# A streaming encoder step: four stretches rearranged, and layer 0's POOL products given to DVE

## The chip, the cores and the metric

The kernel runs on one core of a Trainium2 chip. The metric is the time of one execution on the device in microseconds (us). Three runs of the kernel before took 2004.25, 2011.17 and 2015.48 us; the median is 2011.17.

Engines by their short names: PE is TensorE (PEld its weight loads), DVE is VectorE, ACT is ScalarE, POOL is GpSimd, SP is SyncE, which here issues nearly all DMAs. Each engine runs its own instructions in the order in which the program gives them, and waits at one whose inputs are not there.

## The reference

Two layers over N = 544 tokens (512 of a new stream, 32 of a running one), 2048 channels. Layer 0 is recurrent, layer 1 is stick-breaking attention with 16 heads.

```python
def rms_norm(x, g):
    x32 = x.astype(jnp.float32)
    y = x32 * lax.rsqrt(jnp.mean(x32 * x32, axis=-1, keepdims=True) + EPS) * g.astype(jnp.float32)
    return y.astype(x.dtype)
...
def rec_layer(x, h0, conv_buf, pool_buf, pos0, g, w_in, conv_w, conv_b, w_r, b_r, w_i, b_i, lam,
              pool_w, pool_scale, w_out):
    h = rms_norm(x, g)
    proj = h @ w_in
    xa, ga, xb, gb = jnp.split(proj, [D_RNN, 2 * D_RNN, 2 * D_RNN + D_POOL], axis=-1)
    xa_c, conv_new = causal_conv(xa, conv_buf, conv_w, conv_b)
    ya, h_new = rg_lru(xa_c, h0, w_r, b_r, w_i, b_i, lam)
    yb, pool_new = pool_mix(xb, pool_buf, pos0, pool_w, pool_scale)
    mixed = jnp.concatenate([ya.astype(x.dtype) * jax.nn.silu(ga),
                             yb.astype(x.dtype) * jax.nn.silu(gb)], axis=-1)
    return x + mixed @ w_out, h_new.astype(x.dtype), conv_new.astype(x.dtype), pool_new.astype(x.dtype)
...
def att_layer_prompt(x, g, w_in, w_out):
    B, T, _ = x.shape
    q, k, v, gt = att_inputs(x, g, w_in)
    ...
    return x + (o.astype(x.dtype) * jax.nn.silu(gt)) @ w_out, k, v
```

`rg_lru` is a gated linear recurrence over time: two gates from small block products, then h = a * h + u. A final `rms_norm` closes both streams. The norm's factor of a token (1/rms) can be applied after a product, since it is one number per token; the kernel does that.

## The kernel before, in words

**Tiles.** Channels lie on the 128 partitions, tokens along the free axis. x is 16 rows (tiles of 128 channels x 544 tokens). A full-precision product is three matmuls of 128x272 (`mm3`, L107 to L110) on operands split into a high and a low half: weights into `wh` (ACT, L203) and `wl` (DVE, L204), data into `xh` (ACT, L230 or L501) and `xl` (DVE, L231 or L502). `raw` (L191 to L196) loads a chunk of six weight rows into a `wraw` buffer through SP.

**Units.** The work goes in units of two output tiles. A `plain_unit` multiplies everything directly: chunks part 0, part 1 and the rest (`XP` rows), each for outputs m = 0 and 1. A `unit` gets the first twelve rows' share with seven products in place of eight, from sums of operands that live in the slots T1 to T4: `make` (L277 to L287) forms T1 to T3 from three loaded quarters (L283 to L285, then L230 and L231), `last` (L294 to L300) forms T4 from a fourth (L299). These sums are made once for each product matrix and then serve all its units.

**Order.** It is written by hand: each unit has numbered stages, and `hooks` hang other work on a stage (0 to 3 are the four chunks, 4 and 5 the rests and outputs of a plain unit; (m, c) lies inside a rest). `store` holds a DMA back for two stages (L318), `run` lets it go. Weight splits and evictions are given high priority, so the scheduler can put them ahead of other operations of an engine. What one engine's order becomes is therefore not that of the text alone.

**Opening** (L471 to L514, L648 to L657). Unit 0 of layer 0's input projection runs while x is loaded. `load_x` loads a row and splits it (L501, L502). The norm needs the sum of squares over all 16 rows: ACT squares a row into an `ev` buffer (L483), and PE sums it over channels with five matmuls of 128x2 a row (`rstd_add`, L137). PE records two for each of them, so a row is ten records. At hook 1 of unit 1 `rstd_sums` (L148 to L158) turns the sums into 1/rms, and at hook 2 `rstd_spread` (L168, L170) spreads it over the partitions for `rbc`.

**Layer 0's recurrence.** For each of 16 tiles `front` and `back` run beside the next unit's matmuls. POOL makes two products of 128x548 and 128x544 there (L607, L620) and copies the last states (L619).

**Output projection** (L772 to L829). Its 24 mixed rows come back from DRAM (`mixd`). Unit 0 is plain; the loads, `makes` and `lastload` for the slots T1 to T3 hang on its stages 4 to (1, 6), and unit 1 is the first with seven products. `x2_out` adds the residual (L805, L806), stores `x2d` and `x2g`, and POOL adds the squares (L123) into `sqacc`.

**Attention, head 0** (L1045 to L1050). The first product unit is plain. On its stages hang the loads and sums of x2g's operands (`one`, `two`, `three`) and the norm: `rstd_sums` at 3, the spread and DVE's copy of it into `rbc` (L1050) at 4.

**End** (L1142 to L1177). The last four rows' products are added to x3, in two token halves; ACT squares (L1164), POOL adds (L1165), and the second half waits for its norm before `finish` scales (L1145) and stores (L1146) 16 tiles.

Of the kernel before, what the change touches and what calls it, by code (L numbers as in the profile page):

```python
# [61 lines left out]
def trunk_step(ctx, tc, xT, w_in_rec, w_out_rec, gates, pool_w, vecs, st_h, st_conv, st_pool,  # L62
# [274 lines left out]
    def rest(src, m, accs, starts, hooks):  # L337
# [3 lines left out]
        for c in range(0, n, step):  # L341
            if c:
                run(hooks, (m, c))
            with tc.high_priority():
                hi, lo = wsplit(raw(src[:, 2 * NS + c:2 * NS + c + step]))
            for j in range(step):
                xh, xl = XP[c + j]
                for acc, hs, st in zip(accs, (H1, H2), starts):
                    mm3(acc, hi[:, j, :], lo[:, j, :], xh[:, hs], xl[:, hs], st and c + j == 0, c + j == n - 1)

    def plain_unit(srcs, out, hooks=None, more=True, early=()):
# [12 lines left out]
        for m in range(2):  # L364
            run(hooks, 4 + m)
            if more:
                rest(srcs[m], m, accs[2 * m:2 * m + 2], (False, False), hooks)
# [88 lines left out]
    with ExitStack() as l0:  # L456
# [15 lines left out]
        for s in (B11, B12, B21, B22):  # L472
            fresh(s)
        xraw = []

        rps = two_banks()
        blocks = token_blocks(0, N)
        sqs = {}
# [10 lines left out]
        def load_x(k):  # L489
            xk = T()  # L490
            nc.sync.dma_start(xk, xT[:, k, :])
            gk = vcol("norm_rec", k)
            if k < 2 * NS:
                j = k % NS
                parts = [(XH[s][:, j, :], XL[s][:, j, :], h)
                         for s, h in zip((B11, B12) if k < NS else (B21, B22), (H1, H2))]
            else:
                hi, lo = fresh_row(k - 2 * NS)
                parts = [(hi, lo, slice(0, N))]
            for hi, lo, h in parts:  # L500
                nc.scalar.activation(hi, xk[:, h], AF.Identity, scale=gk)  # L501
                nc.vector.scalar_tensor_tensor(lo, xk[:, h], gk, f(hi), ALU.mult, ALU.subtract)  # L502
            xraw.append(xk)

        def load_rows(k0, k1):
            for k in range(k0, k1):
                load_x(k)
# [79 lines left out]
        def back(n, c):  # L587
# [19 lines left out]
            nc.gpsimd.tensor_tensor(m_, m_, xc, ALU.mult)  # L607
# [12 lines left out]
            nc.gpsimd.tensor_tensor(hs, hs, g[:, :N], ALU.mult)  # L620
# [17 lines left out]
        def late0():  # L638
# [15 lines left out]
        hk = {0: decay_rates, 1: lambda: box.append(rstd_sums(rps, 0, N, [])),  # L654
# [113 lines left out]
    with ExitStack() as l0b:  # L768
# [25 lines left out]
        def x2_out(u, st):  # L794
# [5 lines left out]
            def out(which, bk, addend):  # L800
# [6 lines left out]
                if which % 2:  # L807
                    store(x2d[:, m, :], x)
                    sq_add(m, x)
# [441 lines left out]
```

## Time and profile before

| | |
|---|---|
| three runs, median | 2011.17 us (2004.25 to 2015.48) |
| the profiled execution: its time | 2008.65 us |
| the profiled execution: its span | 2006.9 us |
| matmul records | 15082 |
| DMA | 257.04 MB, 128 GB/s over the span |
| granted PE clock, mean | 0.98 |

The span runs from the first to the last recorded instruction; 1.75 us of the execution's time lie around it. In the rows that follow a group is `line engine operation out<-in shape xcount | busy us, mean ns | idle time before it and what ended it`. A window row is `from:to length`, then busy time (and instructions) of PE, PEld, DVE, ACT and POOL, the granted PE clock, the DMA share and GB/s. A line of waits is `engine operand line <- what it waited for: us in total, times, longest`. A line of the timeline is `start, length, engine, line, operation`.

### The profile page before, as it was taken

Reading aid. Unit: us, or ns where it says so; the run is one execution under the profiler, and the core shown is the slowest. Engines: PE = TensorE matmul, PEld = TensorE weight load, DVE = VectorE, ACT = ScalarE, POOL = GpSimd, SP = SyncE. Lnnn points to the kernel's source line nnn. Section 1 sums busy time; section 2 is a strip of 40 time slices with the busy share of each in tenths; the row PEclk is TensorE's granted clock in tenths of the full one; section 3 lists DMA queues with packets and bytes.
Section 4 is the critical chain, followed back from the end, with each engine's and each line's share of the span. In section 5 each row is a group of like instructions: output and inputs, shape, how many; then the busy total and the mean of one; then the engine's idle time right before and its main releaser. Section 6 shows DMA issues by size and latency. Waiting matters only on the chain.

```text
span 2006.9 us, 37651 instructions
## 1 busy us (share of the span) xinstructions
PE 1941.0 (97%) x15082; PEld 1919.6 (96%) x15082; DVE 1446.4 (72%) x2318; ACT 919.3 (46%) x1284; POOL 261.6 (13%) x369
## 2 busy tenths in 40 slices
PE   8999999999999889999799999999999999999996
PEld 8999999998999789999799999999999999999996
DVE  4465668669888665556788888888888888874347
ACT  5466666665434443334444453444444444442233
POOL 0021113112010000101111110110111101110013
PEclk8899999999999989999899999999999999999998
DMA  5254434333335654446433343333333333365334
GB/s 181 63 157 144 141 117 137 101 88 103 106 105 179 206 151 141 144 142 212 137 101 102 118 126 103 101 112 116 98 105 107 121 106 101 101 213 183 106 99 148
DMA packets 129951, 257.04 MB, mean 128 GB/s; under 512 B 15920, under 2 KB 40752, under 8 KB 129776
## 3 DMA queue, kind: packets, MB, share of 16 engines
q1 hardware_dynamic: 129696, 254.37, 42.0%
q8 instruction: 118, 1.93, 0.4%
q14 instruction: 57, 0.47, 0.1%
q0 software_dynamic: 80, 0.28, 0.0%
HBM read 217.64 MB, written 36.95 MB: 127 GB/s over the span
## 4 chain that ended last, share of the span: by engine, by line
PE 76%; DVE 12%; issue 5%; DMA 5%; ACT 1%; POOL 0%; SPq 0%; DVEq 0%; ACTq 0%; POOLq 0%
PE pp L108 23%; PE pp L110 23%; PE pp L109 23%; DVE wl L204 3%; DMA wraw<-in_w_in_att 2%; PE pg L137 1%; DMA wraw<-in_w_in_rec 1%; DVE xl L231 1%; DMA T<-x2g 1%; PE pm L109 1%; DVE big L898 1%; PE pm L110 1%; PE pm L108 1%; PE pa L915 1%; DVE e L447 1%
## 5 line engine op out<-in xcount | busy, mean ns | idle before, releaser
L108 PE MATMUL pp<-xh,wh 128*128 128x272 f32 x3180 | 925.4, 292 | 21.0 <-ACT xh L230 10.7
L110 PE MATMUL pp<-xh,wl 128*128 128x272 f32 x3180 | 921.3, 290 | 4.2 <-DVE wl L204 3.9
L109 PE MATMUL pp<-xl,wh 128*128 128x272 f32 x3180 | 921.0, 290 | 1.3 <-DVE xl L231 1.3
L203 ACT ACTIVATE wh<-wraw 128x768 fp32r<-128x768 f32 (+2 forms) x622 | 485.1, 782 | 839.5 <-PE pp L109 603.8
L204 DVE TENSOR_TENSOR wl<-wraw,wh 128x768 fp32r<-128x768 f32 (+2 forms) x622 | 546.2, 881 | 240.1 <-ACT wh L203 237.4
L108 PEld LDWEIGHTS pp<-xh,wh 128*128 128x128 f32 x3180 | 605.2, 191 | 23.7 <-ACT xh L230 11.6
L110 PEld LDWEIGHTS pp<-xh,wl 128*128 128x128 f32 x3180 | 604.2, 190 | 7.0 <-DVE wl L204 6.8
L109 PEld LDWEIGHTS pp<-xl,wh 128*128 128x128 f32 x3180 | 605.0, 190 | 3.2 <-DVE xl L231 2.1
L110 PE MATMUL pp<-xp,wl 128*128 128x272 f32 x1152 | 334.3, 290 | 2.5 <-DVE wl L204 2.2
L108 PE MATMUL pp<-xp,wh 128*128 128x272 f32 x1152 | 332.3, 290 | 3.0 <-ACT xp L230 3.0
L109 PE MATMUL pp<-xp,wh 128*128 128x272 f32 x1152 | 332.1, 289 | 0.0
L108 PEld LDWEIGHTS pp<-xp,wh 128*128 128x128 f32 x1152 | 218.9, 191 | 4.4 <-ACT xp L230 3.3
L110 PEld LDWEIGHTS pp<-xp,wl 128*128 128x128 f32 x1152 | 218.8, 190 | 3.6 <-DVE wl L204 3.6
L109 PEld LDWEIGHTS pp<-xp,wh 128*128 128x128 f32 x1152 | 218.3, 190 | 0.2 <-DVE xp L231 0.2
L447 DVE TENSOR_TENSOR e<-pp,e 128x272 f32<-128x272 f32 x156 | 65.6, 438 | 42.5 <-PE pp L110 37.9
L408 DVE TENSOR_TENSOR e<-pp,e 128x272 f32<-128x272 f32 x184 | 75.4, 430 | 5.6 <-PE pp L110 4.6
L109 PE MATMUL pp<-T,wh 128*128 128x272 f32 x256 | 73.0, 288 | 0.0
L110 PE MATMUL pp<-T,wl 128*128 128x272 f32 x256 | 72.9, 287 | 0.0
L108 PE MATMUL pp<-T,wh 128*128 128x272 f32 x256 | 71.9, 288 | 0.0
L230 ACT ACTIVATE xh<-T 128x544 fp32r<-128x544 f32 x72 | 46.5, 654 | 52.7 <-DVE T L283 18.2
L209 ACT ACTIVATE T<-T 128x544 fp32r<-128x544 f32 (+1 forms) x72 | 45.1, 646 | 44.1 <-DMA T<-in_cv 16.1
L231 DVE TENSOR_TENSOR xl<-T,xh 128x544 fp32r<-128x544 f32 x72 | 51.7, 735 | 12.7 <-ACT xh L230 12.5
(242 smaller groups left out, 2141.3 us busy)
## 6 DMA issues: line engine op xcount, KB each, us to landing
wraw<-in_w_in_att SPq DMA_DIRECT2D x128, 384.0 KB, 3.5
wraw<-in_w_in_rec SPq DMA_DIRECT2D x96, 384.0 KB, 3.4
wraw<-in_w_out_rec SPq DMA_DIRECT2D x64, 384.0 KB, 3.4
wraw<-in_w_in_att SPq DMA_DIRECT2D x64, 256.0 KB, 3.3
wraw<-in_w_in_rec SPq DMA_DIRECT2D x48, 256.0 KB, 3.3
wraw<-in_w_out_att SPq DMA_DIRECT2D x32, 384.0 KB, 4.0
T<-in_xT SPq DMA_DIRECT2D x44, 272.0 KB, 4.6
T<-mixd SPq DMA_DIRECT2D x36, 272.0 KB, 4.5
```

The source lines that it names most:

```text
L108: nc.tensor.matmul(out, wh, xh, start=start, stop=False)
L109: nc.tensor.matmul(out, wh, xl, start=False, stop=False)
L110: nc.tensor.matmul(out, wl, xh, start=False, stop=stop)
L137: nc.tensor.matmul(ps[:, 1, 256 + 2 * c:258 + 2 * c], a[:, st:st + P], ones[:, :2], start=first and c == 0, stop=last and c == n - 1)
L203: nc.scalar.activation(hi, src, AF.Copy)
L204: nc.vector.tensor_tensor(lo, src, f(hi), ALU.subtract)
L209: nc.scalar.activation(a, src, AF.Copy)
L230: nc.scalar.activation(h, src, AF.Copy)
L231: nc.vector.tensor_tensor(l, src, f(h), ALU.subtract)
L408: nc.vector.tensor_tensor(sm[name], acc[p], sm[other], ALU.add)
L447: nc.vector.tensor_tensor(src, bk, addend, ALU.add)
L898: nc.vector.tensor_tensor_scan(inc[:, o:o + w][:, ::-1], s, s, 1.0, ALU.mult, ALU.min)
```

## The change

Five edits, none of which alters what is computed.

1. Opening: rows of x are loaded ahead into the space of slots T1 to T3, which is free until unit 10 (`room`), with the weight chunks between them; `early` also feeds the rest chunks. The splits hang on unit 0's stages. Squares are summed by DVE into `sqacc`, and PE sums over channels once.
2. Output projection: unit 1 is plain as well, and the sums' loads and makes hang on its stages; T4 (`three`) is made at stage 0 of unit 2. The squares are added by DVE.
3. Head 0: `rstd_sums` moves from stage 3 to 1, and the copy into `rbc` goes to ACT, with high priority.
4. End: DVE adds the squares, the last two rows' squares stay apart and are summed by PE, and the 16 last stores are issued by SP and ACT in turn.
5. Layer 0's products m*xc and hs*g go from POOL to DVE.

```diff
-    def rest(src, m, accs, starts, hooks):
+    def rest(src, m, accs, starts, hooks, early=()):
...
-                hi, lo = wsplit(raw(src[:, 2 * NS + c:2 * NS + c + step]))
+                hi, lo = wsplit(early.pop(0) if early else raw(src[:, 2 * NS + c:2 * NS + c + step]))
...
+        room = [xs.tile([P, 3, N], F32, tag=f"{q}{s}", name=nm("xraw")) for s in (T1, T2, T3) for q in ("xh", "xl")]
+
+        def load_rows(k0, k1):
+            for k in range(k0, k1):
+                xraw.append(room[k // 3][:, k % 3, :])
+                nc.sync.dma_start(xraw[k], xT[:, k, :])
+
+        def scale_rows(k0, k1):
...
         def squares(k0, k1):
             for k in range(k0, k1):
-                sqs[k] = ev()
-                nc.scalar.activation(sqs[k][:, :N], xraw[k], AF.Square)
-
-        def add_squares(k0, k1):
-            for k in range(k0, k1):
-                rstd_add(rps, blocks, sqs[k], k == 0, k == KT - 1)
...
-        early = [raw(w_in_rec[0, :, :NS])]
-        load_rows(0, 6)
-        early.append(raw(w_in_rec[1, :, :NS]))
-        squares(0, 5)
-        load_rows(6, 8)
-        early.append(raw(w_in_rec[0, :, NS:2 * NS]))
+                sq_add(k, xraw[k], eng=nc.vector)
+
+        def chunk(m, c):
+            early.append(raw(w_in_rec[m, :, c * NS:min((c + 1) * NS, KT)]))
+
+        early = []
+        load_rows(0, 1)
+        chunk(0, 0)
+        load_rows(1, 6)
+        chunk(1, 0)
+        load_rows(6, 9)
+        chunk(0, 1)
+        load_rows(9, 12)
+        chunk(1, 1)
+        load_rows(12, KT)
+        chunk(0, 2)
+        chunk(1, 2)
+        scale_rows(0, 6)
...
-            nc.gpsimd.tensor_tensor(m_, m_, xc, ALU.mult)
+            nc.vector.tensor_tensor(m_, m_, xc, ALU.mult)
...
-            nc.gpsimd.tensor_tensor(hs, hs, g[:, :N], ALU.mult)
+            nc.vector.tensor_tensor(hs, hs, g[:, :N], ALU.mult)
...
-            1: lambda: (add_squares(0, 5), early.append(raw(w_in_rec[1, :, NS:2 * NS])), load_rows(8, 11), squares(5, 9)),
-            2: lambda: (add_squares(5, 9), load_rows(11, 14), squares(9, 13)),
-            3: lambda: (add_squares(9, 13), load_rows(14, 16), squares(13, 16)),
-            4: lambda: add_squares(13, 16)}, early=early)
+            1: lambda: scale_rows(6, 9), 2: lambda: (scale_rows(9, 12), squares(0, 3)),
+            3: lambda: (scale_rows(12, KT), squares(3, 6)), 4: lambda: squares(6, 9),
+            5: lambda: squares(9, 12)}, early=early)
+        squares(12, KT)
...
-                    sq_add(m, x)
+                    sq_add(m, x, eng=nc.vector)
...
-                    4: lambda: (made_rows(), load(), loads[0]()),
-                    (0, 6): lambda: (makes[0](), loads[1]()),
-                    5: lambda: (makes[1](), loads[2]()),
-                    (1, 6): lambda: (makes[2](), lastload())})
+                    4: lambda: (made_rows(), load())})
+            elif u == 1:
+                plain_unit(srcs, out, {
+                    0: loads[0],
+                    1: lambda: (makes[0](), loads[1]()),
+                    2: lambda: (makes[1](), loads[2]()),
+                    3: lambda: makes[2](),
+                    4: load, 5: lastload})
             else:
                 hk = {2: load}
-                if u == 1:
-                    hk[1] = three
+                if u == 2:
+                    hk[0] = three
...
-                with_hooks(ha, {0: [lambda: pend.append(rows(x2g))], 1: [one, lambda: pend.pop()()], 2: [two],
-                                3: [lambda: box.append(rstd_sums(rps, 0, N)), three],
-                                4: [lambda: nc.vector.tensor_copy(rbc, rstd_spread(rps, box[0]))]})
+
+                def spread_rbc():
+                    with tc.high_priority():
+                        nc.scalar.activation(rbc, rstd_spread(rps, box[0]), AF.Copy)
+                with_hooks(ha, {0: [lambda: pend.append(rows(x2g))],
+                                1: [lambda: box.append(rstd_sums(rps, 0, N)), one, lambda: pend.pop()()],
+                                2: [two], 3: [three],
+                                4: [spread_rbc]})
...
-            nc.sync.dma_start(y[:, m, s], o)
+            queue.dma_start(y[:, m, s], o)
...
-                elif m < KT - 1:
+                elif m < KT - 2:
...
-                    nc.gpsimd.tensor_tensor(sqacc[:, s], sqacc[:, s], sq, ALU.add)
+                    nc.vector.tensor_tensor(sqacc[:, s], sqacc[:, s], sq, ALU.add)
...
-            finish(m, 1, r)
+            finish(m, 1, r, (nc.sync, nc.scalar)[m % 2])
```

PE in the opening, where unit 0's second output begins, before. `ev` holds one row's squares, `pp` are the products, `pg` the norm's sums; x5 is one row of x.

```order
L137 MATMUL pg_117<-ones,ev_158 128x2 x5
L108 MATMUL pp_197<-xh_1_109,wh_292 128x272
L137 MATMUL pg_117<-ones,ev_160 128x2 x5
L109 MATMUL pp_197<-xl_2_110,wh_292 128x272
L110 MATMUL pp_197<-xh_1_109,wl_293 128x272
L108 MATMUL pp_198<-xh_3_111,wh_292 128x272
L109 MATMUL pp_198<-xl_4_112,wh_292 128x272
L137 MATMUL pg_117<-ones,ev_162 128x2 x5
```

PE after the change has one such group, behind unit 1's first 36 products:

```order
L108 MATMUL pp_500<-xh_3_111,wh_542 128x272
L109 MATMUL pp_500<-xl_4_112,wh_542 128x272
L110 MATMUL pp_500<-xh_3_111,wl_543 128x272
L137 MATMUL pg_117<-ones,sqacc 128x2 x5
L108 MATMUL pp_501<-xh_1_109,wh_601 128x272
L109 MATMUL pp_501<-xl_2_110,wh_601 128x272
```

Sixteen groups among unit 0's products became one that reads `sqacc`.

DVE at head 0 before, from the last T1 to T3 sums on. `rs` are the norm's five small numbers per token block, `big` the diagonal tiles that the spread multiplies.

```order
L283 TENSOR_TENSOR T_11024<-T_11024,T_11020 128x544
L151 TENSOR_TENSOR rs_74<-rs_73 128x5
L299 TENSOR_TENSOR T_11117<-T_11117,xh_1575_11086 128x544
L284 TENSOR_TENSOR T_11020<-T_11020,T_11022 128x544
L231 TENSOR_TENSOR xl_1578_11089<-T_11024,xh_1577_11088 128x544
L285 TENSOR_TENSOR T_11022<-T_11024,T_11022 128x544
L231 TENSOR_TENSOR xl_1574_11085<-T_11020,xh_1573_11084 128x544
L152 SCALAR_TENSOR_TENSOR rs_74<-rs_74,rs_71 128x5
L299 TENSOR_TENSOR T_11117<-T_11117,xl_1576_11087 128x544
L231 TENSOR_TENSOR xl_1576_11087<-T_11022,xh_1575_11086 128x544
L153 SCALAR_TENSOR_TENSOR rs_73<-rs_74,rs_73 128x5
```

DVE at head 0 after the change, the same chain and what follows it:

```order
L150 RECIPROCAL rs_73<-rs_72 128x5
L151 TENSOR_TENSOR rs_74<-rs_73 128x5
L152 SCALAR_TENSOR_TENSOR rs_74<-rs_74,rs_71 128x5
L153 SCALAR_TENSOR_TENSOR rs_73<-rs_74,rs_73 128x5
L158 TENSOR_SCALAR big_10932<-ident,rs_73 128x128 x5
L231 TENSOR_TENSOR xp_10957<-T_10871,xp_10956 128x544
L231 TENSOR_TENSOR xp_10961<-T_10873,xp_10960 128x544
L231 TENSOR_TENSOR xp_10965<-T_10875,xp_10964 128x544
L204 TENSOR_TENSOR wl_11160<-wraw_11157,wh_11159 128x512
L231 TENSOR_TENSOR xp_10969<-T_10877,xp_10968 128x544
L283 TENSOR_TENSOR T_10942<-T_10942,T_10938 128x544
```

The norm's chain, spread before among the operand sums, stands in one piece ahead of the first of them (L283).

SP in the output projection before, at the residual's loads from `in_xT` for unit 0. The tiles T from `mixd` of 128x2x272 are the quarters for the operand sums; `x2d` and `x2g` are unit 0's stores.

```order
L798 DMA T_7946<-in_xT 128x544
L798 DMA T_7947<-in_xT 128x544
L237 DMA T_7950<-mixd 128x2x272
L237 DMA T_7952<-mixd 128x2x272
L237 DMA T_7954<-mixd 128x2x272
L326 DMA x2d<-T_7946 128x544
L326 DMA x2d<-T_7947 128x544
L195 DMA wraw_8488<-in_w_out_rec 128x768
L195 DMA wraw_8530<-in_w_out_rec 128x768
L237 DMA T_8013<-mixd 128x2x272
L237 DMA T_8015<-mixd 128x2x272
```

SP at the same place after the change:

```order
L802 DMA T_7875<-in_xT 128x544
L802 DMA T_7876<-in_xT 128x544
L195 DMA wraw_8494<-in_w_out_rec 128x768
L326 DMA x2d<-T_7875 128x544
L326 DMA x2d<-T_7876 128x544
L195 DMA wraw_8496<-in_w_out_rec 128x768
L326 DMA x2g<-T_7966 128x544
L237 DMA T_8065<-mixd 128x2x272
L237 DMA T_8067<-mixd 128x2x272
L237 DMA T_8069<-mixd 128x2x272
L195 DMA wraw_8498<-in_w_out_rec 128x768
```

The quarters' loads moved behind unit 0's stores, with unit 1's weight chunks between them.

More of the change, by code (lines that the diff above doesn't have):

```diff
@@ L366, in plain_unit @@
             if more:
-                rest(srcs[m], m, accs[2 * m:2 * m + 2], (False, False), hooks)
+                rest(srcs[m], m, accs[2 * m:2 * m + 2], (False, False), hooks, early)
             for hf in range(2):
@@ L473, in trunk_step @@
             fresh(s)
+        rps = two_banks()
         xraw = []
-        rps = two_banks()
-        blocks = token_blocks(0, N)
-        sqs = {}
+        room = [xs.tile([P, 3, N], F32, tag=f"{q}{s}", name=nm("xraw")) for s in (T1, T2, T3) for q in ("xh", "xl")]
[4 more added lines that the diff above has]
+        def scale_rows(k0, k1):
+            for k in range(k0, k1):
+                xk, gk = xraw[k], vcol("norm_rec", k)
+                if k < 2 * NS:
+                    j = k % NS
+                    parts = [(XH[s][:, j, :], XL[s][:, j, :], h)
+                             for s, h in zip((B11, B12) if k < NS else (B21, B22), (H1, H2))]
+                else:
+                    hi, lo = fresh_row(k - 2 * NS)
+                    parts = [(hi, lo, slice(0, N))]
+                for hi, lo, h in parts:
+                    nc.scalar.activation(hi, xk[:, h], AF.Identity, scale=gk)
+                    nc.vector.scalar_tensor_tensor(lo, xk[:, h], gk, f(hi), ALU.mult, ALU.subtract)
@@ L1140, in trunk_step, with finish @@
         pend.pop()()
-        def finish(m, hf, r):
+        def finish(m, hf, r, queue=nc.sync):
             s = (H1, H2)[hf]
@@ L1145, in finish @@
             nc.vector.scalar_tensor_tensor(o, o, vcol("norm_final", m), r, ALU.mult, ALU.mult)
-            nc.sync.dma_start(y[:, m, s], o)
+            queue.dma_start(y[:, m, s], o)
         for hf, s in enumerate((H1, H2)):
+            accs = [sqacc]
             for m in range(KT):
@@ L1161, in trunk_step @@
                     nc.scalar.activation(sqacc[:, s], x3[m][:, s], AF.Square)
-                elif m < KT - 1:
+                elif m < KT - 2:
                     sq = e()
                     nc.scalar.activation(sq, x3[m][:, s], AF.Square)
-                    nc.gpsimd.tensor_tensor(sqacc[:, s], sqacc[:, s], sq, ALU.add)
+                    nc.vector.tensor_tensor(sqacc[:, s], sqacc[:, s], sq, ALU.add)
                 else:
-                    last = T()
-                    nc.scalar.activation(last[:, s], x3[m][:, s], AF.Square)
-                    accs = [sqacc, last]
+                    accs.append(T())
+                    nc.scalar.activation(accs[-1][:, s], x3[m][:, s], AF.Square)
                 if hf == 1 and m >= 8:
```

23 lines of the change are left out of this document (3 added, 20 removed).

## The prediction

> **What bounds the kernel now.** I read the page first, for the busy shares and the chain that ended last.
>
> ```profile
> span 2006.9 us, 37651 instructions
> PE 1941.0 (97%) x15082; PEld 1919.6 (96%) x15082; DVE 1446.4 (72%) x2318; ACT 919.3 (46%) x1284; POOL 261.6 (13%) x369
> ```
>
> TensorE (PE) is busy 97% of the span, so little seems left. But busy is not fast. The windows of 25 us tell more, by the number of matmuls in each and by the granted clock (the last figures of a row are clock, DMA share and GB/s).
>
> ```profile
> 25.00:50.00 25.00, 25.00 (x166) 25.00 (x167) 8.73 (x20) 12.13 (x23) 0.19 (x1) 0.77 0.35 116
> 50.00:75.00 25.00, 25.00 (x157) 25.00 (x156) 5.26 (x14) 6.69 (x12) 0.00 (x0) 0.73 0.17 52
> 700.00:725.00 25.00, 17.89 (x93) 16.50 (x93) 16.97 (x28) 9.47 (x14) 0.00 (x0) 0.75 0.58 171
> 725.00:750.00 25.00, 25.00 (x202) 25.00 (x201) 15.87 (x23) 10.30 (x15) 2.90 (x2) 1.00 0.44 133
> 975.00:1000.00 25.00, 13.85 (x85) 13.64 (x86) 22.21 (x42) 9.92 (x15) 2.10 (x3) 0.66 0.18 56
> 100.00:300.00 200.00, 200.00 (x1599) 200.00 (x1598) 123.49 (x192) 131.67 (x172) 39.18 (x49) 1.00 0.48 139
> ```
>
> A good stretch does 202 matmuls in 25 us, 0.1238 us each; that is my unit of account. Three places fall short: the opening (clock 0.77 and 0.73 though PE is busy all the time), the start of the output projection about 700 us, and head 0 of the attention about 975 us. The end is the fourth place. Elsewhere PE runs at its rate, and only PE time removed shortens the span.
>
> **The opening.** These are two PE groups between 7 and 76 us, one burst of L137, the end of the spread that closes the stretch, two windows of 2 us in it, and a single burst of ten L137 records at head 0 with the window behind it.
>
> ```profile
> L108 PE MATMUL pp<-xh,wh 128*128 128x272 f32 x72 | 24.4, 351 | 7.3 <-ACT xh L501 7.3
> L137 PE MATMUL pg<-ones,ev 128*128 128x2 f32 x160 | 23.2, 270 | 0.0
> 19.01 1.73 PE L137 MATMUL pg<-ones,ev 128*128 128x2 f32 x10
> 75.88 0.31 PE L170 MATMUL pg<-big,ones 128*128 128x32 f32 x2
> 8.00:10.00 2.00, 2.00 (x9) 1.80 (x9) 2.00 (x6) 2.00 (x6) 0.00 (x0) 1.00 1.03 403
> 24.00:26.00 2.00, 2.00 (x10) 2.00 (x10) 0.00 (x0) 0.00 (x0) 0.00 (x0) 0.50 0.00 0
> 960.55 1.17 PE L137 MATMUL pa<-ones,sqacc 128*128 128x2 f32 x10
> 962.00:972.00 10.00, 10.00 (x82) 10.00 (x81) 6.89 (x13) 5.84 (x9) 0.00 (x0) 1.00 0.96 301
> ```
>
> PE works from 7.25 to 76.19 us, 68.9 us, on 264 products (192 of unit 0: 16 rows, two outputs, two halves, three products; and unit 1's first 72), 160 L137 records and the spread. The products alone are 264 x 0.1238 = 32.7. L137 at full clock is 160 x 0.117 = 18.7 (ten in 1.17). The spread, ten records as well, is about 1.2, and the slow first matmuls (9 in 2 us at the start) cost about 2.3 more. Together 54.9; the missing 14.0 is half clock without an idle gap, as in the window 24 to 26, behind groups like that at 19.01. One burst of ten at 960.55 is followed by ten microseconds at 1.00, so ten alone don't lower the clock. After the change there is one burst of ten. PE's work is then 32.7 + 1.2 + 1.2 + 2.3 = 37.4; begun at 7.25 as before it ends at 44.6, a gain of 31.5 if nothing waits.
>
> What could wait is the burst on sqacc, since DVE now adds the squares. These rows price DVE's work ahead of it:
>
> ```profile
> L502 DVE SCALAR_TENSOR_TENSOR xl<-T,vec,xh 128x272 fp32r<-128x272 f32 x24 | 10.3, 495 | 4.8 <-ACT xh L501 4.8
> L204 DVE TENSOR_TENSOR wl<-wraw,wh 128x768 fp32r<-128x768 f32 x4 | 3.8, 954 | 2.4 <-ACT wh L203 2.4
> L204 DVE TENSOR_TENSOR wl<-wraw,wh 128x512 fp32r<-128x512 f32 x2 | 1.4, 692 | 13.2 <-ACT wh L203 13.2
> L502 DVE SCALAR_TENSOR_TENSOR xp<-T,vec,xp 128x544 fp32r<-128x544 f32 x2 | 1.5, 780 | 0.1
> L283 DVE TENSOR_TENSOR T<-T,T 128x544 f32<-128x544 f32 x3 | 2.2, 724 | 7.5 <-DMA T<-mixd 7.5
> ```
>
> DVE has 10.3 for xl, 3.0 for four xp rows, about 5.2 for unit 0's weights and 1.9 for unit 1's first two, and 15 adds of 0.64 to 0.72 (L283 has their shape), 10 to 11: 30 to 31 from about 7, so 37 to 38.4 without a pause. PE reaches the burst at 7.25 + 2.3 + 228 x 0.1238 = 37.8. I take 1.5 us of waits, there and at the borders between weight chunks, where a schedule by hand from these prices leaves DVE 1 to 2 us: **30** gained. Bounds: 32, and 22 if each of the five borders costs 2 us, which is what DVE would need for two or three operations out of turn.
>
> [...]
>
> **The output projection.** PE's waits between 690 and 724, DVE's longest, and the stretch from the first to the last of these gaps:
>
> ```profile
> PE pp L108 <- ACT xh L230: 10.4, 3, 4.6
> PE pp L108 <- DVE T L806: 1.0, 1, 1.0
> PE pp L110 <- DVE wl L204: 0.8, 1, 0.8
> DVE T L283 <- DMA T<-mixd: 7.5, 2, 4.1
> 690.60:722.40 31.80, 19.04 (x95) 17.38 (x94) 22.32 (x37) 14.11 (x21) 1.87 (x1) 0.79 0.57 168
> ```
>
> Unit 1's operand sums (L283 to L285, L230, L231) wait for loads from mixd. In 31.8 us PE does 95 matmuls, worth 11.8: 20.0 lost, 12.8 in gaps and the rest at half clock. After the change unit 1 is a plain unit on rows that exist, and loads and sums go to its hooks, one unit earlier than their use. It needs 288 matmuls for 270: -2.2. At unit 2 the sums of T4 wait for the last load behind x2d's stores on SP; my trace by hand gives about 2. So 20.0 - 2.2 - 2 = **16**. Upper bound 18; lower 6, if waits like the 7.5 and some 4 us of slow matmuls behind them come back at unit 2. The square adds go to DVE at 0.7 each in the stretch behind, where DVE is at 15.9 of 25: nothing.
>
> **The norm copy at head 0.**
>
> ```profile
> PE pa L168 <- issue: 11.8, 1, 11.8
> PE pp L108 <- DVE T L449: 2.0, 1, 2.0
> 978.44 0.16 DVE L151 TENSOR_TENSOR rs<-rs 128x5 f32<-128x5 f32 x1
> 983.75 1.06 DVE L158 TENSOR_SCALAR big<-ident,rs 128x128 f32<-128x128 f32 x5
> 972.30:997.20 24.90, 11.07 (x66) 10.95 (x66) 22.35 (x42) 9.90 (x15) 2.10 (x3) 0.66 0.17 54
> ```
>
> The 11.8 put down to issue is PE holding the spread until L158, whose small ancestors stand between L283, L299 and L231 on DVE (order rows above). The 24.9 us hold 54 products (6.7) and the spread (1.1): 17.1 lost. After the change L137 comes after 36 matmuls, the chain L150 to L158 stands in one piece, and ACT copies rbc. The operand work of 0.7 each does not shrink: DVE is at 22.4 of 24.9 here, and the T2 operands, behind the x2g loads, are ready about 980.5 by hand, when PE could want them at 977 to 979. I subtract 4: **13**. Upper 16; lower 6, if that DVE queue still ends last.
>
> **The end.**
>
> ```profile
> PE pa L137 <- POOL sqacc L1165: 2.5, 1, 2.5
> L1145 DVE SCALAR_TENSOR_TENSOR big<-big,vec,rbc 128x272 f32<-128x272 f32 x6 | 3.9, 684 | 0.0
> 1988.28 0.42 DVE L1159 TENSOR_TENSOR big<-big,pp 128x272 f32<-128x272 f32 x1
> 1988.63 1.97 DVE L1145 SCALAR_TENSOR_TENSOR big<-big,vec,rbc 128x272 f32<-128x272 f32 x3
> 1999.50 2.54 DVE L1145 SCALAR_TENSOR_TENSOR big<-big,vec,pa 128x272 f32<-128x272 f32 x6
> 1995.93 4.75 SPq L1146 DMA_DIRECT2D out_y<-T  x10
> 2000.78 3.12 SPq L1146 DMA_DIRECT2D out_y<-big  x6
> ```
>
> The 2.5 is not POOL's alone: DVE's last additions stand behind L1145s of 0.66 each (three in 1.97), against 0.42 where POOL is idle (six in 2.54). In the last half 13 adds, at 0.42 as L1159 has it, come to DVE (+5.5), and 16 L1145 get up to 0.24 cheaper (-3.8): 1.7 lost, or less where other DVE work is eased too. Sixteen stores take 7.9 us to issue, 0.49 each, against DVE's 16 x 0.42 = 6.8; two queues leave 1.1. The sum over POOL's last add, 2.5, goes in part. **1**, between -3 (no relief from POOL, the 2.5 stays) and +4 (the 2.5 and the 1.1 whole).
>
> [...]
>
> **POOL's products in layer 0.**
>
> ```profile
> L608 DVE SCALAR_TENSOR_TENSOR ev<-big,ev 128x548 f32<-128x548 f32 x8 | 5.8, 730 | 27.2 <-ACT ev L606 27.2
> L619 POOL COPY ho<-T x16: 187/188/1003, 102.1 to 486.0; 128x2 f32<-128x2 f32 x16
> ```
>
> From 100 to 300 us, eight units, DVE is idle 76.5, 9.6 a unit. m*xc (0.72) falls in the 3.4 that DVE waits before L608; hs*g (0.72) stands behind POOL's copy of ho (0.19 to 1.0), with L449 and the next wl behind it. At most 2.5 of 9.6: **0**, from -2 to +3 for the few full stretches.
>
> **Sum.** 30 + 16 + 13 + 1 + 0 = 60 off the profiled execution's 2008.65: 1948.7. That execution lies 2.5 below the median of the runs, 2011.17, so by the median 1951. I say 1949, nearer to the sum's own basis. The terms' bounds add to 22 + 6 + 6 - 3 - 2 = 29 and 32 + 18 + 16 + 4 + 3 = 73.
>
> **The rivals.** First: the half clock has another cause than the L137 groups. [...] Then the opening's 14.0 stay, the gain is 46, the time 1963. For it: no run here separates them; against it: the window 24 to 26 comes behind L137 groups, and the 200 us from 100 on, without them, are at 1.00. Second: new waits take the old ones' place where the rearranged loads stand, at unit 2 and at head 0, since SP and DVE work in order and DVE is nearly full there: 6 + 6 for 16 + 13, 1966. For it: 22.4 of 24.9 on DVE; against: the chain of five small operations no longer waits between them. Third, slower: DVE's wait for POOL at hs*g holds the next wl. It decides once a unit's waits pass the 9.6 us of DVE idle less 1.4 of new work, 8.2; to turn the sum past +10 us it must cost PE 70 / 16 = 4.4 a unit, a wait of 12.6 where the longest copy shows 1.0; at 4.6 a unit the time is 2011 - 60 + 74 = 2025. Fourth: the gains are hidden by something that the profile does not show (about 2009); against it, all four are gaps or slow matmuls of the engine that sets the span.
>
> **How the numbers follow.** Forecast 0.74 (1937 to 1960), the first rival 0.09, the second 0.11, the third 0.02, the fourth 0.04. A measurement of this kernel can tell about 0.5%, 10 us, from no change. Faster 0.93, same 0.04, slower 0.03. The range from 1936 to 1972 leaves out the last two and the tails.
>
> **What would show it.** Right: the window 25 to 50 with over 195 matmuls at clock 1.00 and L168 of the first spread ending about 45; no wait over 2 us at units 1 and 2 of the output projection, now 31 us earlier, about 660 to 695; the spread at head 0 with no wait over 2 us; and out_y issues on two queues. Wrong: clock under 0.9 after 15 us, PE waiting for sqacc by over 3 us, waits <-ACT xh L230 at unit 2, or PE waits <-DVE wl in layer 0 that recur in each unit.

## The result, and the profile after

The changed kernel takes 1948.85 us (median of 4 runs, 1947.40 to 1951.53), the kernel before 2009.39 (4 runs, 2004.25 to 2015.48). The ratio is 0.970, with a 95% interval from 0.967 to 0.973. Forecast were 1949 us and a range from 1936 to 1972. The sum came out; its terms less so. (One later execution of the changed kernel took 3107.76 us at a mean granted clock of 0.56, a slow state of the core, and is left out everywhere below.)

To see where the time came from I set the two timelines side by side by products, not by time. PE does 13764 products into `pp` before and 13782 after (18 more in the output projection's unit 1). The n-th product of one kernel is the n-th of the other up to there, and behind it, counted from the end. The difference of their start times is what has been gained so far:

| place | start before, us | gained up to it | gained in the stretch ahead | forecast |
|---|---|---|---|---|
| behind the opening (product 500) | 108.7 | 31.0 | 31.0 | 30 |
| the output projection's unit 1 (product 4750) | 690.2 | 35.9 | 4.9 | 0 |
| behind the output projection | 899.8 | 49.8 | 13.9 | 16 |
| behind head 0 | 1051.2 | 56.7 | 7.0 | 13 |
| the last products' start | 1921.7 | 56.1 | -0.6 | 0 |
| the span's end | 2006.9 | 57.2 | 1.1 | 1 |

The stretch called layer 0 below runs from product 500 to 4750; its last 288 products are the output projection's unit 0.

(The profiled execution of the changed kernel is the slowest of its four runs, 1951.53, span 1949.7; hence 57.2 here and 60.5 between the medians.)

The page's first lines:

```profile
span 1949.7 us, 37295 instructions
PE 1908.4 (98%) x14962; PEld 1886.8 (97%) x14962; DVE 1469.1 (75%) x2390; ACT 915.6 (47%) x1281; POOL 176.6 (9%) x294
```

The windows of 25 us that answer to those of before:

```profile
25.00:50.00 25.00, 25.00 (x203) 24.82 (x202) 21.63 (x56) 15.44 (x27) 1.05 (x3) 1.00 0.34 95
50.00:75.00 25.00, 25.00 (x202) 25.00 (x201) 19.34 (x31) 19.11 (x26) 2.00 (x5) 1.00 0.36 103
650.00:675.00 25.00, 23.34 (x185) 23.00 (x184) 14.06 (x21) 9.29 (x14) 0.00 (x0) 1.00 0.69 222
925.00:950.00 25.00, 21.95 (x151) 21.76 (x152) 24.20 (x39) 11.94 (x18) 3.47 (x2) 0.86 0.38 118
```

The opening now runs at its rate: 203 matmuls where 166 stood, clock 1.00. The output projection has no half clock any more. Head 0 (925 to 950) still has some, 0.86. PE's waits over the whole span, the larger ones:

```profile
PE pp L108 <- ACT wh L203: 7.4, 2, 7.1
PE pp L110 <- DVE wl L204: 4.8, 7, 1.1
PE pp L108 <- DVE T L449: 3.1, 1, 3.1
PE pg L108 <- ACT T L209: 2.2, 3, 1.2
PE pa L137 <- DVE sqacc L1179: 2.2, 1, 2.2
PE pp L108 <- ACT xp L230: 2.0, 1, 2.0
PE pp L108 <- DVE T L810: 1.7, 1, 1.7
```

The 11.8 put down to issue is gone, as are the 10.4 <-ACT xh L230. The 3.1 <-DVE T L449 stands at head 0. The opening's burst and the spread behind it:

```profile
38.28 1.28 PE L137 MATMUL pg<-ones,sqacc 128*128 128x2 f32 x10
44.00 1.05 PE L168 MATMUL pg<-big,ones 128*128 128x128 f32 x8
44.89 0.31 PE L170 MATMUL pg<-big,ones 128*128 128x32 f32 x2
```

The spread ends at 45.20, against 76.19 before and the forecast's "about 45"; PE reached the burst at 38.3 and did not wait for `sqacc`.

### The profile page after: what moved, and what is told of

Read it like the earlier page. It is cut to its first block, busy times and chain, and to the rows that moved or that the text cites. A ratio compares the mean times of both kernels' runs of the same rounds, so it can differ in the third digit from the quotient of the medians.

```text
span 1949.7 us, 37295 instructions
## 1 busy us (share of the span) xinstructions
PE 1908.4 (98%) x14962; PEld 1886.8 (97%) x14962; DVE 1469.1 (75%) x2390; ACT 915.6 (47%) x1281; POOL 176.6 (9%) x294
## 4 chain that ended last, share of the span: by engine, by line
PE 76%; DVE 12%; DMA 6%; issue 4%; ACT 2%; POOL 0%; SPq 0%; DVEq 0%; POOLq 0%; ACTq 0%
PE pp L108 23%; PE pp L110 23%; PE pp L109 23%; DVE wl L204 4%; DMA wraw<-in_w_in_att 2%; DVE big L906 1%; DMA T<-mixd 1%; DMA T<-x2g 1%; DVE xl L231 1%; PE pm L109 1%; PE pm L110 1%; PE pm L108 1%; ACT wh L203 1%; PE pa L923 1%; DVE e L447 1%
## 5 line engine op out<-in xcount | busy, mean ns | idle before, releaser
L204 DVE TENSOR_TENSOR wl<-wraw,wh 128x768 fp32r<-128x768 f32 (+2 forms) x619 | 541.4, 878 | 187.3 <-ACT wh L203 180.5
L230 ACT ACTIVATE xh<-T 128x544 fp32r<-128x544 f32 x72 | 46.6, 655 | 53.0 <-DVE T L283 15.8
L231 DVE TENSOR_TENSOR xl<-T,xh 128x544 fp32r<-128x544 f32 x72 | 50.5, 721 | 12.4 <-ACT xh L230 12.3
```

The costliest lines, as they stand in the source:

```text
L204: nc.vector.tensor_tensor(lo, src, f(hi), ALU.subtract)
L230: nc.scalar.activation(h, src, AF.Copy)
L231: nc.vector.tensor_tensor(l, src, f(h), ALU.subtract)
```

## The experiments

Each stretch's gain is read by products, as in the table above, against the kernel before. Most are single executions. The kernel before took 2010.54 us beside `open_alone`, `wide`, `out_alone` and `norm_alone`, 2013.87 beside `pool_alone`, `no_pool`, `end_alone` and `norm_early`, 2014.03 (median of 7) beside `pool_dummy` and `norm_mix`, 2010.58 (median of 11) beside the last two; single executions of it lie between 2004.25 and 2020.36, so the readings by products carry the argument, not the times.

**open_alone**: the opening's lines of the diff, nothing else.

> The kernel before with the opening's edit alone. Theory: the opening gains 31 us by itself (PE's 264th product ends at about 45 us instead of 76) and nothing later moves, so the span is 2006.9 - 31 = 1976. Rival: part of what the whole change gained in the opening hangs on another edit, or the earlier start runs into other waits in layer 0, so the span is above 1980.

Measured: 1985.87 us, span 1984.2. The opening itself gained 30.8, so the term stands by itself. But 8 of it were given back behind: 3.7 in layer 0, 0.3 in the output projection, 0.5 at head 0 and 3.7 in the attention behind it, where the clock stays at 1.00 and PE is idle for 7.8 us instead of 4.6. What happens in layer 0 is to be seen in two windows around the same wait of 1.7 us <-DVE big (L584, L588 in the changed text), the kernel before first, then open_alone.

```profile
330.00:340.00 10.00, 8.34 (x67) 8.12 (x66) 7.63 (x12) 6.83 (x10) 2.79 (x2) 1.00 0.50 141
```

```profile
300.00:310.00 10.00, 8.31 (x52) 7.94 (x51) 7.08 (x11) 6.52 (x9) 1.90 (x2) 0.83 0.53 133
```

The idle time is the same, 1.7 us. In one kernel the clock stays at 1.00, in the other it falls, and 15 matmuls (1.9 us) are lost on top. So the rival was right as to the span: an earlier start meets the same waits at another moment, and the price of a wait is not fixed. The last section shows on what it depends.

**wide**: the L137 matmuls of the opening with 48 moving columns, not 2.

```diff
-            nc.tensor.matmul(ps[:, 1, 256 + 2 * c:258 + 2 * c], a[:, st:st + P], ones[:, :2],
+            nc.tensor.matmul(ps[:, 1, 256 + wd * c:256 + wd * (c + 1)], a[:, st:st + P], ones[:, :wd],
...
-                rstd_add(rps, blocks, sqs[k], k == 0, k == KT - 1)
+                rstd_add(rps, blocks, sqs[k], k == 0, k == KT - 1, 48)
```

> The kernel before with one number changed in the opening: the norm's L137 matmuls have 48 moving columns, not 2 (48 equal sums for one). Theory: the half clock comes from matmuls that hardly occupy the array; with 48 columns the clock stays near 1.00 from 15 to 76 us, the records take the same 0.117 us each, and the spread ends 14 us earlier, at about 62; span 1993. Rival: the half clock has another cause (the weight loads of L137, or the traffic of the opening): the windows stay at 0.73 to 0.77, the spread ends at 76 or later, span 2007 or more.

Measured: 1998.13 us, span 1996.4; the opening gained 11.9. Its windows:

```profile
14.00:30.00 16.00, 16.00 (x113) 16.00 (x112) 8.31 (x30) 8.76 (x18) 0.00 (x0) 0.79 0.50 165
25.00:50.00 25.00, 25.00 (x214) 25.00 (x213) 9.18 (x18) 13.95 (x25) 0.19 (x1) 1.00 0.35 108
50.00:75.00 25.00, 25.00 (x203) 25.00 (x202) 12.00 (x24) 9.48 (x16) 1.40 (x3) 1.00 0.23 64
```

From 25 us on the clock is 1.00 where it was 0.77 and 0.73, with the same 160 records. They do not stand in the same places: with this edit the scheduler put the first 40 behind product 36 in one piece, where the kernel before has groups of ten behind products 36, 37, 41 and 45. So the run by itself does not part the columns from the order. Two stretches of 3.41 us with nearly equal work do, before first, then `wide`, each with the stretch that follows it (why 3.41, the last section says):

```profile
29.68:33.09 3.41, 3.41 (x31) 3.41 (x31) 1.28 (x6) 1.06 (x2) 0.00 (x0) 1.00 0.37 68
33.09:36.51 3.42, 3.42 (x18) 3.42 (x17) 0.92 (x2) 1.68 (x4) 0.00 (x0) 0.50 0.96 359
```

```profile
28.01:31.42 3.41, 3.41 (x31) 3.41 (x31) 2.06 (x5) 2.34 (x6) 0.00 (x0) 1.00 0.47 94
31.42:34.83 3.41, 3.41 (x30) 3.41 (x30) 1.03 (x3) 1.59 (x4) 0.00 (x0) 1.00 1.01 375
```

In both first stretches 10 products start; beside them 20 records of two columns in the one, 19 of 48 columns in the other. Half clock follows the first and not the second, so the two moving columns lowered the clock. Between 14 and 30 us `wide` is still at 0.79: there stands the piece of 40, and in 3.41 us without any product 48 columns do not hold the clock either.

```profile
14.15 3.94 PE L137 MATMUL pg<-ones,ev 128*128 128x48 f32 x33
```

**out_alone**: the output projection's lines and the squares on DVE.

> The kernel before with the output projection's edit alone (unit 1 plain, sums on its stages, squares on DVE). Theory: its gain is its own: 13 to 14 us at equal products, as in the whole change, span 1993. Rival: the forecast's 16 holds for the edit alone and the other edits took 2 of it, span 1991; or the gain needs the others, span above 1998.

Measured: 1994.20 us, span 1992.5; 13.9 gained in the stretch by equal products. The first theory holds. The waits that remain, in this kernel from product 4750 (690.3 us) on:

```profile
PE pp L108 <- DVE T L806: 1.6, 1, 1.6
PE pp L110 <- DVE wl L204: 1.6, 2, 1.2
```

**norm_alone**: head 0's lines.

> The kernel before with head 0's edit alone. The whole change gained 7 us there where I forecast 13. Theory: the missing 6 are the edit's own (T loads land late, DVE then is full, the first unit's evictions L449 stand behind the sums): 7 us here too, with a wait <-DVE T L449 of about 3 us, span 2000. Rival: another edit takes them (squares on DVE ahead of the chain, or the earlier arrival): 11 to 13 us here, span 1995.

Measured: 2005.64 us, span 2003.9. Head 0 gained about 9, from 4.2 behind to 4.5 ahead. That lies between the two expectations, and the waits there are others than in the whole change:

```profile
PE pa L137 <- POOL sqacc L123: 1.7, 1, 1.7
PE pp L108 <- ACT xh L230: 1.4, 1, 1.4
PE pp L108 <- ACT wh L203: 0.4, 1, 0.4
```

No wait for L449, and half clock for one stretch of 3.4 us alone, behind the 1.7 (959.15 to 962.57, clock 0.50). So the 3.1 us of the whole change do not belong to the edit as such. This kernel was also 2.1 us later than the kernel before already at product 250, where the two programs are the same; see the last section.

**pool_alone**: L607 and L620 on DVE.

> The kernel before with the two products of layer 0's recurrence on DVE and nothing else. The whole change gained 4.9 us between the opening and the output projection, where I forecast 0. [...] Rival: the gain comes from the other arrival times after the opening's edit; then 0 to 1 here, span 2006, or a loss.

Measured: 2005.47 us, span 2003.8; I had expected 2002, and 4 to 6 us as this edit's own gain. Layer 0 gained 5.6 up to product 4500, in three steps: 2 us about 330 us, 2 about 460 and 1.4 about 495, where PE's waits <-DVE big L584 and <-DVE wl L204 had been. 2.0 were given back in the output projection, 1.6 of them ahead of product 4750. So the gain is this edit's own, and the rival falls. How POOL costs DVE time is in these rows, POOL's product and the DVE operation beside it in the kernel before, then the same DVE stretch in this one:

```profile
310.24 1.59 POOL L607 TENSOR_TENSOR big<-big,ev 128x548 f32<-128x548 f32 x1 [2.46 <-ACT big L597]
...
310.52 1.89 DVE L231 TENSOR_TENSOR xl<-T,xh 128x544 fp32r<-128x544 f32 x1
```

```profile
310.61 0.72 DVE L607 TENSOR_TENSOR big<-big,ev 128x548 f32<-128x548 f32 x1
311.25 0.72 DVE L231 TENSOR_TENSOR xl<-T,xh 128x544 fp32r<-128x544 f32 x1
```

DVE's own operation took 1.89 us beside POOL's product, and 0.72 without; it ended 0.58 us behind POOL's, as if it had stood still for the rest. Doing the product itself costs DVE 0.64 here, running beside POOL's cost it 1.17. That is not so beside every product: from 80 to 640 us POOL made 32 in the kernel before, ten DVE operations were slowed beside them, by 9 us in all, and L449, which reads PSUM, took its 0.43 beside them too. In `pool_alone` and in the changed kernel no DVE operation is slowed there.

**pool_dummy**: the changed kernel with two products more on POOL in each of layer 0's tiles, into a scratch tile that nobody reads; they are extra work.

```diff
+            nc.gpsimd.tensor_tensor(scr, xc[:, :N], rbc, ALU.mult)
             nc.vector.tensor_tensor(m_, m_, xc, ALU.mult)
...
+            nc.gpsimd.tensor_tensor(scr, g[:, :N], rbc, ALU.mult)
             nc.vector.tensor_tensor(hs, hs, g[:, :N], ALU.mult)
```

> The changed kernel with two products of 128x544 more on POOL in each of layer 0's sixteen tiles, into a scratch tile that nobody reads. Theory: POOL's products slow DVE while they run (a DVE operation beside one took 1.89 us in the kernel before, 0.72 without), so layer 0 loses the 5 to 9 us again that the edit gained there: span 1955 to 1959, waits <-DVE wl and <-DVE big back. Rival: the gain came from the products' results being there earlier on DVE; products that nobody waits for cost nothing: span 1949 to 1951.

Measured: 1953.52 us, span 1951.7. From product 500 to 4000 it lost 0.3 where the changed kernel gained 5.6, and 1.7 already before product 500. PE's waits <-DVE big and <-DVE wl are back, smaller (1.7 and 0.8 between 80 and 600 us; the changed kernel has none there). The theory holds for the place: products that nobody reads cost 6 us there, so it was not the results' earlier arrival. The span, 1951.7, lies under the 1955 expected: it is 2.0 above the first profile of the changed kernel and 7.3 above its second (below). The difference is head 0, which gained 10.2 here and 7.0 and 9.8 in those; the output projection gained 13.6.

**no_pool**: the whole change without those two products.

> The whole change without the two products of layer 0 on DVE (they stay on POOL). The opening's edit alone gave back 3 us of its 31 in layer 0. Theory: without POOL's products on DVE this comes back: the span is 1949.7 + 5 to 8 = 1955 to 1958, with waits of PE <-DVE wl and <-DVE big in layer 0. Rival: the products' place is indifferent (my forecast's 0): 1949 to 1951.

Measured: 1953.53 us, span 1951.8. Layer 0 lost 2.0 in place of gaining 4.9, and the waits <-DVE big and <-DVE wl are back (2.9 and 2.8 between 80 and 600 us), so the theory holds there, at 7 us. The span, 1951.8, misses the 1955 to 1958 expected: 2.1 of the 7 are left against the first profile of the changed kernel and 7.4 against its second (below).

**end_alone**: the end's lines.

> The kernel before with the end's edit alone. Forecast 1 us, the whole change showed 1 there. Theory: about 1 here, span 2005.9, DVE without a gap up to the last addition as before. Rival: with POOL gone DVE's scalings take 0.42 and not 0.66, and the end gains up to 4, span 2003.

Measured: 2004.35 us, span 2002.6, of which 2.7 were gained in the opening, whose program is that of before; 1.6 are left for the end and the scatter of the attention. The first theory holds, within a scatter of half a microsecond: in five runs of the kernel before with other edits the same stretch moved by -0.5 to +0.2. In the changed kernel the last scalings beside no POOL work take the shorter time, and DVE has no gap up to the last sum all the same:

```profile
1933.34 0.92 DVE L1158 SCALAR_TENSOR_TENSOR big<-big,vec,rbc 128x272 f32<-128x272 f32 x2
1934.16 0.44 DVE L1173 TENSOR_TENSOR big<-big,pp 128x272 f32<-128x272 f32 x1
1934.51 0.92 DVE L1158 SCALAR_TENSOR_TENSOR big<-big,vec,rbc 128x272 f32<-128x272 f32 x2
1936.70 0.16 DVE L148 TENSOR_SCALAR rs<-pa 128x3 f32<-128x3 f32 x1 [1.28 <-PE pa L137]
```

Two in 0.92, or 0.46, where three took 1.97. From the last products to L148, behind the last sum, the changed kernel takes 0.5 us longer all the same, the additions on DVE included; from L148 to the end it takes 13.0 in place of 14.6, since the last stores now go out on two queues.

**norm_early**: the changed kernel with head 0's nine loads for the sums ahead of the four rows.

```diff
-                with_hooks(ha, {0: [lambda: pend.append(rows(x2g))],
-                                1: [lambda: box.append(rstd_sums(rps, 0, N)), one, lambda: pend.pop()()],
+                with_hooks(ha, {0: [one, lambda: pend.append(rows(x2g))],
+                                1: [lambda: box.append(rstd_sums(rps, 0, N)), lambda: pend.pop()()],
```

> The changed kernel, with the nine loads for head 0's operand sums issued ahead of the four last rows' loads and one stage earlier. Theory: the 6 us that head 0 gained less than forecast come from late loads: DVE stands idle for them and is then full when the first unit's evictions (L449) are due, PE waits 3.1 us and runs 5 us at half clock. With earlier loads the wait falls under 1 us and the gain there goes from 7 to 10 or 12; span 1945. Rival: DVE's sums are the bound whatever the loads do, or the rows that the running unit needs now land late: no change or slower, 1949 to 1955.

Measured: 1946.66 us, span 1944.8. Head 0 gained 10.1, the wait for L449 and the half clock are gone, and a wait of 2.7 <-ACT xp L230 is new: the rows land late. Both expectations are right in part.

**norm_mix**: two groups of the sums' loads first, then the rows, then the third group.

```diff
-                with_hooks(ha, {0: [lambda: pend.append(rows(x2g))],
-                                1: [lambda: box.append(rstd_sums(rps, 0, N)), one, lambda: pend.pop()()],
-                                2: [two], 3: [three],
+                with_hooks(ha, {0: [loads[0], loads[1], lambda: pend.append(rows(x2g))],
+                                1: [lambda: box.append(rstd_sums(rps, 0, N)), loads[2], lambda: pend.pop()()],
+                                2: [*makes, lastload], 3: [three],
```

> The changed kernel with head 0's loads in a third order: two of the three groups for the operand sums ahead of the four last rows, the third behind. Theory: both waits at head 0 (3.1 us <-DVE T L449 with the rows first, 2.7 <-ACT xp L230 with all sums first) are late loads on SP's one queue; between the two orders both shrink, head 0 gains 12 of the forecast's 13 or more, span 1942 to 1944. Rival: SP's queue is full there, one of the two waits always stays at 2 to 3 us: span 1944.8 to 1950.

Measured: 1945.33 us (4 runs, 1943.65 to 1946.26), ratio to the kernel before 0.965, interval 0.963 to 0.967; span 1943.1. The waits at head 0 shrank to three of 0.6 or less:

```profile
PE pp L108 <- ACT xp L230: 0.6, 1, 0.6
PE pp L109 <- DVE xp L231: 0.6, 2, 0.4
PE pp L109 <- DVE xl L231: 0.6, 1, 0.6
```

Head 0 gained 10.3, less than the 12 expected: over the whole stretch PE is still idle for 2.8 us, and one stretch of 3.4 us at half clock behind the first of these waits (920.01 to 923.42, clock 0.50) cost 1.7 more.

**best**: norm_mix, and unit 0's two residual rows in the output projection loaded at stage 2 instead of 4.

> The changed kernel with head 0's loads in the mixed order and, in the output projection, unit 0's two residual rows loaded two stages earlier. Theory: PE's wait of 1.7 us for a PSUM bank (<-DVE T L810) stands behind these late loads; it goes, so the time is 1 to 2 us under the mixed order's 1945.3: 1943 to 1944.5, ratio to the kernel before about 0.965. Rival: the earlier loads push back the mixed rows on SP's queue, a wait <-ACT T L230 takes the place: 1945 to 1947.

Measured: 1946.51 us (4 runs), ratio 0.967, interval 0.966 to 0.969; span 1943.7. The wait <-DVE T L810 is gone, and 0.6 each <-ACT T L230 and <-DVE T L231 came in its place: the rival. The output projection gained 16.0, but the stretch ahead, where the loads now stand, 4.8 in place of norm_mix's 6.4. It is not shown to be faster than norm_mix.

**after_again**: the changed kernel once more, on the same chip.

> The changed kernel itself, once more beside the one above on the same chip: 1947 to 1952, ratio to the kernel before 0.967 to 0.973. A second profile of it shows how much of the ledger by products differs from run to run: within 1 us in the opening if the clock stays at 1.00 there, where the kernel before moved by up to 3.

Measured: 1946.29 us (median of five runs, 1945.59 to 1947.49), ratio 0.967, interval 0.966 to 0.969; span 1944.4. So neither `best` nor `norm_mix` is shown to beat the changed kernel: their intervals overlap with this one. In this profile head 0 gained 9.8, not 7.0. PE's waits there in the first profile, and windows of 4 us behind the first of them:

```profile
PE pp L108 <- DVE T L449: 3.1, 1, 3.1
PE pp L108 <- ACT wh L203: 0.4, 1, 0.4
```

```profile
924.00:928.00 4.00, 0.85 (x6) 0.66 (x5) 4.00 (x8) 1.66 (x4) 0.00 (x0) 0.87 0.66 231
928.00:932.00 4.00, 4.00 (x19) 4.00 (x19) 4.00 (x7) 2.05 (x4) 2.53 (x2) 0.50 0.19 70
932.00:936.00 4.00, 4.00 (x27) 4.00 (x27) 4.00 (x7) 2.33 (x4) 0.94 (x1) 0.78 0.57 165
```

The same in this profile, waits and then windows of 6 us:

```profile
PE pp L108 <- DVE T L449: 2.0, 1, 2.0
PE pp L108 <- ACT xh L230: 1.4, 1, 1.4
PE pp L108 <- ACT wh L203: 0.4, 1, 0.4
```

```profile
924.00:930.00 6.00, 5.26 (x42) 5.29 (x43) 6.00 (x12) 3.48 (x6) 3.48 (x2) 1.00 0.17 61
930.00:936.00 6.00, 4.58 (x36) 4.36 (x36) 6.00 (x10) 2.42 (x4) 4.90 (x1) 1.00 0.39 122
```

Together PE waits about as long, 3.5 and 3.8 us. In one piece of 3.1 us it is followed by half clock: 46 matmuls from 928 to 936, worth 5.7 us, in 8. In two pieces of 2.0 and 1.4 it is not. `norm_early` has a single wait of 2.7 us and no half clock behind it, so the number of pieces does not decide it (last section).

## Why the prediction was right, step by step

**The opening** (30, measured 31.0 in the whole change and 30.8 alone) was right in mechanism and size. The rival that the half clock has another cause fell with `wide`: the same records with 48 columns gave back 12 of the 14 us that I had put down to it, and at equal work per stretch half clock follows the narrow records alone. PE shows as 100% busy in the rows all the while: 25.00 of 25.00 us in the kernel before's windows at 0.77 and 0.73.

**The output projection** (16, measured 13.9 in the whole change and 13.9 alone) had its mechanism right: no half clock is left in the stretch, and PE's idle time there fell from 12.8 to 3.1. I had subtracted 2 for new waits; 1.7 <-DVE T L810 and 1.4 <-DVE wl L204 came. The first is not new in kind (1.0 <-DVE T L806 stood there before), nor is the second (0.8): I had counted both old ones as gone. That is 1 of the missing 2; the other stays open.

**Head 0** (13, measured 7.0 and 9.8 in two profiles) is the mis-sized term. The chain of the norm no longer waits, as forecast: the burst comes after 36 products and the spread 26 later without a gap. I subtracted 4 for the operand sums. Of the 17.1 us lost before, 10 are still lost in the one profile and 7 in the other. Of these PE's idle time makes 5.1 and 5.0, half clock 3.0 and nothing; 2 us in each are not accounted for. The largest wait comes since DVE stands idle for the sums' loads (2.5 us up to 917.6, and several shorter waits ahead) and then is full when the first unit's evictions are due, 924 to 927. My step "T2 operands ready about 980.5" looked at the sums alone, and left out that L449 stands in the same queue and that a wait of 3 us can bring half clock behind it (here 3.1, and clock 0.50 from 928 to 932). `norm_early` and `norm_mix` show that the order of the loads decides which of the waits comes; even with all of them at 0.6 or less 10.3 were gained, so 13 was too much for this edit in any order that was run.

**The end** (1, measured 1.1 and about 1.6 alone): right in size, and nearly in its parts. The two queues gave 1.6 where I had 1.1; the work up to the last sum cost 0.5, where I had 1.7 lost on DVE and part of the 2.5 of waiting won back. That wait is still there, as 2.2 <-DVE sqacc L1179.

**POOL's products** (0 with a range from -2 to +3, measured in layer 0 as 4.9 and 5.9 in two profiles of the whole change and 4.0 alone): the step that failed is "at most 2.5 of 9.6: 0". I added DVE's new work and did not subtract what DVE had lost beside POOL, though the same effect carried my end term (0.66 against 0.42 for a scaling). In a stretch with idle time that does not show; in the full stretches at 330, 460 and 495 us it was 1.4 to 2 us each. What DVE loses is in the row of 1.89 us against 0.72; by what mechanism, no run shows. That the gain is DVE's time and not the results' arrival is shown by `pool_dummy`. How much of it stays in the span is not settled: 3.1 in `pool_alone`, 2.1 or 7.4 by `no_pool`, 2.0 or 7.3 by `pool_dummy`. That something stays is likely: `no_pool` and `pool_dummy` took 1953.5 in their one execution each, and the nine executions of the changed kernel that are compared here took 1945.59 to 1951.53.

So the total was near by luck in part: 4.9 too little for POOL's products met 6 too much for head 0 and 2 too much for the output projection.

## What to carry to other kernels

A PE that is 100% busy can still run at half clock (3.42 of 3.42 us busy at 0.50, with 18 matmuls where the stretch ahead had 31): count matmuls per window and read the granted clock, and keep tiny matmuls in one burst (of ten records in the changed opening, whose windows stand at 1.00). POOL work beside a DVE that is full is not free: the DVE operation shown lost 1.17 us beside a product of 1.59. Where a stretch is full, give DVE the product (5.6 us in layer 0 in `pool_alone`). When parts of a change are added up, compare timelines by product number: it shows each part's gain in that execution to a tenth of a microsecond, and what the next stretch gives back. One execution is not enough for it: head 0's gain differed by 2.8 us between two profiles of the same kernel.

## What the runs showed of the hardware that I had not expected

The price of a PE wait depends on when it falls. A wait of 1.7 us cost 1.7 in the kernel before and about 3.5 in `open_alone`. The traces show why. In each of the fourteen every change of the granted clock, between 1.00 and 0.50, lies on one grid of 3.41 us (in the kernel before those at 19.44, 29.68, 33.09, 39.92 and 50.16 us are 3, 1, 2 and 3 times 3.41 apart), and this grid lies elsewhere against the program's start in each execution (29.68 us is on it before, 28.01 in `wide`). Two stretches of the grid around that wait, before first, then `open_alone`:

```profile
330.05:333.46 3.41, 1.97 (x16) 1.74 (x14) 3.41 (x6) 1.51 (x2) 0.55 (x1) 1.00 0.53 163
333.46:336.88 3.42, 3.21 (x25) 3.21 (x26) 3.42 (x6) 2.25 (x4) 0.25 (x1) 1.00 0.42 120
```

```profile
299.98:303.40 3.42, 1.73 (x12) 1.36 (x12) 3.42 (x6) 1.51 (x2) 0.55 (x1) 1.00 0.43 129
303.40:306.81 3.41, 3.41 (x17) 3.41 (x17) 3.41 (x6) 1.88 (x3) 0.00 (x0) 0.50 0.44 115
```

In the kernel before the wait falls into two stretches of the grid, 14 matmuls start in the first, and nothing follows. In `open_alone` it falls into one, 10 start, and the next stretch runs at half clock, which costs half of 3.41, 1.7 us. Over all fourteen traces, in the 5924 stretches in which nothing but products of 128x272 and L137 records of two columns starts (a full stretch holds 28 products): fewer than 10 products, and half clock always followed; 13 or more, and full clock always followed; from 10 to 12 both occur. So in these traces it is the products started in a stretch that count, and a wait, or groups of tiny matmuls, cost more when they take enough of one stretch. At head 0 2.4 of the 3.1 us fell into one stretch with 6 products; 2.0 and 1.4 fell into two with 13 and 14; `norm_early`'s 2.7 was cut by the grid into 1.9 and 0.8.

The kernel before is unsteady for the same reason. Four kernels here have its opening unchanged, with PE's operations in the same order, and their product 250 stands at -0.1, -2.1, 0.0 and +2.7 us against the first profile (`out_alone`, `norm_alone`, `pool_alone`, `end_alone`). The stretches of the grid at half clock in this opening number 9 in the kernel before, and 9, 11, 9 and 7 in these. The changed opening, at clock 1.00, stands at 30.8 to 31.0 in seven profiles (`pool_dummy`, with its extra work, left out). Removing the half clock has removed that scatter too.
